# Seven block products for eight in one quad of each layer-A pair, with helper splits held back in ScalarE's queue

## The chip, the cores and the metric

One core of one Trainium2 chip runs the kernel. The metric is device time in microseconds (us) of one execution. The kernel before took 1844.6 us (median of three runs, 1844.6 to 1847.14). Engines are named as the profile names them: PE (TensorE, matmuls), PEld (its weight loads), ACT (ScalarE), DVE (VectorE), POOL (GpSimd) and SP (SyncE, here only an issuer of DMAs).

## The reference

Two layers over 256 tokens of width 2048, inner width 4096, 32 heads of 128, all in float32.

```python
h = rms_norm(x, a_norm)                       # layer A
q, k, v, g = split(h @ a_w_in, 4)             # 2048 -> 4 x 4096
o = chunked_relbias_attention(q, k, v)        # per head
x = x + (o * silu(g)) @ a_w_out               # 4096 -> 2048
h_kv = rms_norm(x, kv_norm)                   # layer B
k, v = split(h_kv @ kv_w, 2); logf = log_sigmoid(h_kv @ f_w + f_b)
q, g = split(rms_norm(x, b_norm) @ b_w_in, 2)
x = x + (forgetting_attention(q, k, v, cumsum(logf)) * silu(g)) @ b_w_out
return rms_norm(x, final_norm)
```

## The kernel before

**Units.** Every projection is cut into units of 512 output columns. In layer A a *pair* of units belongs to two heads (a group, `g` = 0 to 15): unit `aqk` gives their q and k, unit `avg` their v and gate. The contraction of 2048 is 16 blocks of 128, taken two at a time, so a unit has eight *steps*. A float32 product is made of three float32r products: x and w are each split into a high part (`xTh`, `aqk_hi`) and the rest (`xTl`, `aqk_lo`), and `mm3` (L160) issues hi·hi, hi·lo and lo·hi. With two tiles of 128 tokens (`NT`), a step is 2 x 2 x 3 = 12 matmuls of 128x512, a unit 96.

**The feed.** `Feed` (L171) streams the weights. SP loads a raw block pair of 512 KB (three slots, `RAW`), ACT copies it to the high part (L216), DVE subtracts to get the low part (L217), and both go into a ring of four (`SPLIT`): the split of step n+4 starts when PE has finished step n, and the load n+3 when DVE has finished split n.

**The side work.** The attention of a group is a generator (`attention`, L353) that `drive` (L519) advances at given steps of the units that run meanwhile (`QK_STEPS`, `PV_STEPS`). Its stages, in the order in which one group goes through them:

1. at the end of unit `aqk`: ACT scales q and k out of PSUM into `qk` (L335);
2. first step of `avg`: `turn` (L321) transposes 32x32 blocks on DVE into `qkY` and moves the blocks by 16 DMAs, all issued by POOL, into `qkZ`;
3. late in `avg`: the turned rows are split on ACT and DVE (`wideh`, `widel`, `q1h`, `q1l`, `q0`), then PE makes the scores `s1p`, `s0p` after the last step of `avg`;
4. in the next group's `aqk`: softmax on DVE and ACT (`sg`), times the gate, a second `turn` (`sgY`, 16 DMAs of POOL, `sgZ`), and `wideh`, `widel` again;
5. after the first step of the next `avg`: PE multiplies by v (`op`), DVE by the gate (`oT`, L409), ACT and DVE split it into `oAh`, `oAl`.

`qkZ` and `sgZ` share one buffer, so POOL cannot start stage 2 of a group before `oT` of the group before has read `sgZ`.

**Order.** Each engine's queue is in order. The order in a queue is set by a scheduler that takes the program's dependences and its own estimate of times; instructions that wait for nothing late may be placed ahead of others that stand earlier in the source.

Of the kernel before, what the change touches and what calls it, by code (L numbers as in the profile page):

```python
# [9 lines left out]
F32 = mybir.dt.float32  # L10
# [53 lines left out]
def trunk(ctx, tc, x, x_t, gains, a_w_in, a_rel, a_w_out, kv_w, f_w, f_b, b_w_in, b_w_out, final_norm, out):  # L64
# [94 lines left out]

    def mm3(acc, lhs, k, ts, hi, lo, nk):  # L160

        parts = [(lhs.h(k), hi), (lhs.h(k), lo), (lhs.l(k), hi)]
        steps = [(t, i) for t in ts for i in range(3)]
        if k < KB:
            steps = [(t, i) for i in (0, 2, 1) for t in ts]
        for t, i in steps:
            x, w = parts[i]
            pe.matmul(acc[t], x[:, t * P:(t + 1) * P], w,  # L168
                      start=k == 0 and i == 0, stop=k == nk - 1 and i == 2)

    class Feed:  # L171
# [20 lines left out]
        def begin(self, first=None):  # L192
            spec, b = next(self.todo, (None, 0))
            if spec:
                load, *splits = self.also.get((spec["name"], b), (None, None, None))
                if load:
                    load()
                self.loaded.append((spec, b, self.load(spec, b, first), splits))

        def prepare(self, ahead=True, parts=(slice(None),)):  # L200
            if not self.loaded:
                self.begin()
            if not self.loaded:
                return
            spec, b, raw, (before, behind) = self.loaded.pop(0)
            if before:
                before()
            nm, h = spec["name"], b - (spec["nk"] // KB - spec["late"])
            if 0 <= h < spec["kept"]:
                both = big_tile([P, 2, KB, UN], F32R, f"{nm}_keep{b}")  # L210
                hi, lo = both[:, 0], both[:, 1]
            else:
                hi = stream.tile([P, KB, UN], F32R, name=f"{nm}_hi{b}", tag="hi", bufs=SPLIT)
                lo = stream.tile([P, KB, UN], F32R, name=f"{nm}_lo{b}", tag="lo", bufs=SPLIT)
            for j in parts:
                act.activation(hi[:, j], raw[:, j], AF.Copy)  # L216
                self.splits.append(dve.tensor_sub(lo[:, j], raw[:, j], r32(hi[:, j])))  # L217
            if behind:
                behind()
            self.ready.append((hi, lo))  # L220
            while ahead and len(self.loaded) < RAW:
                n = len(self.loaded)
                self.begin()
                if len(self.loaded) == n:
                    break

        def fill(self):
# [18 lines left out]
    for g in range(NG):  # L246
        qkvg.append(spec(f"aqk{g}", a_w_in[2 * g], KD))
        qkvg.append(spec(f"avg{g}", a_w_in[2 * g + 1], KD))
    woven = [(qkvg[u], b) for u, b in WOVEN]
    todo = woven + [i for i in whole(qkvg[1]) if i not in woven]  # L250
    ao = [spec(f"ao{u}", a_w_out[u], KI) for u in range(4)]
    for sp_ in qkvg[2:] + ao:
        todo += whole(sp_)
# [13 lines left out]
    class Unit:  # L267
# [3 lines left out]
        def __init__(self, lhs, sp_):  # L271
            self.lhs, self.nk, self.late = lhs, sp_["nk"], sp_["late"]
            self.acc = [ps_acc.tile([P, UN], F32, name=f"{sp_['name']}_acc{t}", tag="acc") for t in range(NT)]
            self.held, self.left = [], self.nk // KB

        def step(self, b):
            hi, lo = feed.get()
            hold = b >= self.nk // KB - self.late
            if hold:
                self.held.append((b, hi, lo))  # L280
            for j in range(KB):
                mm3(self.acc, self.lhs, b * KB + j, range(1 if hold else NT), hi[:, j], lo[:, j], self.nk)
            self.left -= 1
            if not self.left:
                for b, hi, lo in self.held:
                    for j in range(KB):
                        mm3(self.acc, self.lhs, b * KB + j, [1], hi[:, j], lo[:, j], self.nk)

# [31 lines left out]

    def turn(src, n, name, queues=(pool, pool)):  # L321

        y = att.tile([P, NQ, n, SQ], F32, name=f"{name}Y", tag="Y")
        dve.transpose(y, src.rearrange("p n (j u) -> p j n u", u=SQ))  # L326
        z = att.tile([P, NQ, n, SQ], F32, name=f"{name}Z", tag="Z")
        for i in range(NQ):
            for j in range(NQ):
                queues[j % 2].dma_start(out=z[j * SQ:(j + 1) * SQ, i], in_=y[i * SQ:(i + 1) * SQ, j])  # L330
        return z
# [4 lines left out]

    def split(srcs, tag):
# [14 lines left out]

    def attention(g, biases, qk, vg, half, ocat, queues=(pool, pool)):  # L353

# [84 lines left out]

    for i in range(EXTRA):  # L440
        both = big_tile([P, 2, KB, UN], F32, name=f"early{i}")
        feed.early += [both[:, 0], both[:, 1]]
    xT = Stat("xT", KD)
    xr, homes = {}, iter(["wideh", "tb", "widel", "oT", "gs", "R", "Y", "Z", "wideh"])
    sq = [big_tile([P, BIG, S], F32, name=f"sq{i}") for i in range(KD // BIG)]

# [46 lines left out]
    oA = Stat("oA", KI)  # L493

    def side_a(g, accs):
        tb = att.tile([P, HG, S], F32, name="tb", tag="tb")
# [9 lines left out]
        qk = rows(UN, "qk")  # L506
        evac_scaled(accs["qk"], 0, UN, rsA, qk)
        yield
# [3 lines left out]

        yield from attention(g, biases, qk, vg, halfA, oA, (pool, pool) if g else (pool, act))

    def close_vg(accs):
        accs["v"] = v_split(accs["vg"], 0, rsA)
        accs["g"] = gate_from(accs["vg"], GC, halfA)
# [23 lines left out]
    for g in range(NG):  # L541
        accs = {}
        if g:
            accs["qk"], vg = drive(unit(xT), prev, PV_STEPS), unit(xT)
        else:
# [4 lines left out]
        advance(prev)  # L550
        accs["vg"] = drive(vg, prev, QK_STEPS if g else {0: 1, 5: 1, 6: 2}, old=old)
        close_vg(accs)
# [249 lines left out]
```

## Time and profile before

| what | value |
|---|---|
| median of three runs | 1844.6 us (1844.6 to 1847.14) |
| the profiled execution | 1843.38 us |
| its span | 1841.7 us |
| PE busy | 1830.1 us, 99% |
| PEld busy | 1523.0 us, 83% |
| DVE busy | 1121.7 us, 61% |
| ACT busy | 1005.6 us, 55% |
| POOL busy | 543.5 us, 30% |
| DMA | 396 MB, mean 215 GB/s |
| granted PE clock | 0.999 |

PE's share is near the whole span, but the records of matmuls overlap (each is shown with some 390 ns and the next starts earlier), so the price of a matmul is the distance between starts and not its duration. The other engines work beside PE; for them the question is at which moment in a group's round of some 46 us their result is wanted.

### The profile page before, as it was taken

How to read it: one execution, taken by the hardware profiler on the slowest of the kernel's cores; microseconds unless marked ns; L12 is line 12 of the kernel's file. 1: busy time of each engine (PE TensorE's matmuls, PEld its weight loads, DVE VectorE, ACT ScalarE, POOL GpSimd, SP SyncE). 2: the span in 40 equal slices, each digit the busy share in tenths (PEclk: the TensorE clock that was granted, in tenths of full speed). 3: DMA queues.
4: the chain of work that ended last, by engine and by line, in shares of the span. 5: the costliest groups of instructions: out<-in, count | busy, mean ns of one | idle time of the engine just before them, and what ended most of it. 6: DMA issues, size and time to landing. Idle time of an engine off the chain costs nothing.

```text
span 1841.7 us, 25094 instructions
## 1 busy us (share of the span) xinstructions
PE 1830.1 (99%) x8387; PEld 1523.0 (83%) x8387; DVE 1121.7 (61%) x1433; ACT 1005.6 (55%) x1695; POOL 543.5 (30%) x1127
## 2 busy tenths in 40 slices
PE   9999999999999999999999999999999999999998
PEld 7888888888888888888888888888888888888886
DVE  6666666666666666556655566666665666665654
ACT  6555555555555555454546565555555655554443
POOL 1333333333333333111103333333333333333000
PEclk9999999999999999999999999999999999999999
DMA  7766666666767666677756666666766766677664
GB/s 255 235 217 214 212 214 215 214 213 212 216 214 214 215 214 214 209 226 227 230 190 220 214 216 213 214 214 215 217 212 213 220 213 210 215 237 220 206 205 161
DMA packets 142241, 396.31 MB, mean 215 GB/s; under 512 B 31104, under 2 KB 35744, under 8 KB 141984
## 3 DMA queue, kind: packets, MB, share of 16 engines
q1 hardware_dynamic: 106960, 354.25, 61.6%
q0 software_dynamic: 34048, 39.13, 6.5%
q8 instruction: 66, 1.08, 0.3%
q10 hardware_dynamic: 1104, 1.34, 0.2%
q14 instruction: 63, 0.52, 0.1%
HBM read 351.05 MB, written 4.23 MB: 193 GB/s over the span
## 4 chain that ended last, share of the span: by engine, by line
PE 97%; DVE 1%; DMA 1%; ACT 0%; issue 0%; ACTq 0%; SPq 0%; DVEq 0%
PE bkv_acc L168 19%; PE bqg_acc L168 19%; PE avg_acc L168 18%; PE aqk_acc L168 18%; PE bo_acc L168 9%; PE ao_acc L168 9%; PE op L405 1%; PE s0p L371 1%; PE op L351 0%; PE s1p L351 0%; PE s1p L350 0%; PE op L350 0%; PE op L349 0%; PE s1p L349 0%; DMA avg_raw<-in_a_w_in 0%; DMA xr<-in_x_t 0%
## 5 line engine op out<-in xcount | busy, mean ns | idle before, releaser
L330 POOL DMA_DIRECT2D sgZ<-sgY x512 | 251.5, 498 | 435.2 <-DVE sgY L326 364.1
L330 POOL DMA_DIRECT2D qkZ<-qkY x504 | 247.9, 499 | 399.1 <-DVE vl L424 147.2
L217 DVE TENSOR_TENSOR bqg_lo<-bqg_raw,bqg_hi 128x1024 fp32r<-128x1024 f32 x128 | 156.0, 1222 | 121.3 <-ACT bqg_hi L216 121.3
L217 DVE TENSOR_TENSOR avg_lo<-avg_raw,avg_hi 128x1024 fp32r<-128x1024 f32 x127 | 154.0, 1219 | 110.8 <-ACT avg_hi L216 105.4
L217 DVE TENSOR_TENSOR bkv_lo<-bkv_raw,bkv_hi 128x1024 fp32r<-128x1024 f32 x128 | 155.6, 1219 | 87.6 <-ACT bkv_hi L216 87.6
L216 ACT ACTIVATE bqg_hi<-bqg_raw 128x1024 fp32r<-128x1024 f32 x128 | 135.3, 1058 | 128.3 <-PE bqg_acc L168 67.8
L217 DVE TENSOR_TENSOR aqk_lo<-aqk_raw,aqk_hi 128x1024 fp32r<-128x1024 f32 x125 | 151.5, 1219 | 84.6 <-ACT aqk_hi L216 84.5
L168 PE MATMUL aqk_acc<-aqk_hi,xTh 128*128 128x512 f32 x512 | 195.8, 392 | 0.5 <-ACT aqk_hi L216 0.5
L168 PE MATMUL bkv_acc<-bkv_hi,xkvh 128*128 128x512 f32 x512 | 195.7, 392 | 0.0
L168 PE MATMUL avg_acc<-avg_hi,xTh 128*128 128x512 f32 x512 | 195.7, 392 | 0.0
L168 PE MATMUL bqg_acc<-bqg_hi,xbh 128*128 128x512 f32 x512 | 195.5, 392 | 0.0
L216 ACT ACTIVATE avg_hi<-avg_raw 128x1024 fp32r<-128x1024 f32 x127 | 133.1, 1057 | 113.3 <-PE avg_acc L168 54.2
L168 PE MATMUL aqk_acc<-aqk_lo,xTh 128*128 128x512 f32 x512 | 194.1, 389 | 0.5 <-DVE aqk_lo L217 0.5
L168 PE MATMUL avg_acc<-avg_lo,xTh 128*128 128x512 f32 x512 | 194.1, 389 | 0.4 <-DVE avg_lo L217 0.4
L168 PE MATMUL bkv_acc<-bkv_hi,xkvl 128*128 128x512 f32 x512 | 194.4, 390 | 0.0
L168 PE MATMUL aqk_acc<-aqk_hi,xTl 128*128 128x512 f32 x512 | 194.4, 390 | 0.0
L168 PE MATMUL bqg_acc<-bqg_hi,xbl 128*128 128x512 f32 x512 | 194.3, 390 | 0.0
L168 PE MATMUL avg_acc<-avg_hi,xTl 128*128 128x512 f32 x512 | 194.3, 390 | 0.0
L168 PE MATMUL bkv_acc<-bkv_lo,xkvh 128*128 128x512 f32 x512 | 194.1, 389 | 0.0
L168 PE MATMUL bqg_acc<-bqg_lo,xbh 128*128 128x512 f32 x512 | 194.1, 389 | 0.0
L216 ACT ACTIVATE bkv_hi<-bkv_raw 128x1024 fp32r<-128x1024 f32 x128 | 134.8, 1057 | 76.2 <-PE bqg_acc L168 61.3
L216 ACT ACTIVATE aqk_hi<-aqk_raw 128x1024 fp32r<-128x1024 f32 x125 | 131.0, 1056 | 81.4 <-PE aqk_acc L168 40.1
(188 smaller groups left out, 3430.3 us busy)
## 6 DMA issues: line engine op xcount, KB each, us to landing
bqg_raw<-in_b_w_in SPq DMA_DIRECT2D x128, 512.0 KB, 4.2
bkv_raw<-in_kv_w SPq DMA_DIRECT2D x128, 512.0 KB, 3.5
avg_raw<-in_a_w_in SPq DMA_DIRECT2D x127, 512.0 KB, 4.3
aqk_raw<-in_a_w_in SPq DMA_DIRECT2D x125, 512.0 KB, 3.8
ao_raw<-in_a_w_out SPq DMA_DIRECT2D x64, 512.0 KB, 4.4
bo_raw<-in_b_w_out SPq DMA_DIRECT2D x64, 512.0 KB, 4.2
sgZ<-sgY POOLq DMA_DIRECT2D x512, 40.0 KB, 4.0
qkZ<-qkY POOLq DMA_DIRECT2D x504, 32.0 KB, 3.3
```

Source lines behind the costliest of these rows:

```text
L168: pe.matmul(acc[t], x[:, t * P:(t + 1) * P], w, start=k == 0 and i == 0, stop=k == nk - 1 and i == 2)
L216: act.activation(hi[:, j], raw[:, j], AF.Copy)
L217: self.splits.append(dve.tensor_sub(lo[:, j], raw[:, j], r32(hi[:, j])))
L330: queues[j % 2].dma_start(out=z[j * SQ:(j + 1) * SQ, i], in_=y[i * SQ:(i + 1) * SQ, j])
L371: pe.matmul(s0p[:, i], q0[:, i], qkT[:, HG + i, 0], start=True, stop=True)
L405: pe.matmul(op[:, i, P:], v1[:, i * DH:(i + 1) * DH], pT[:, i, NT], start=False, stop=i == HG - 1)
```

## The change

In the last two blocks of the contraction, a pair of units is a product of a 2x2 grid of x blocks (two blocks of the contraction, two token tiles) and a 2x2 grid of weight blocks (two blocks, units `aqk` and `avg`): eight block products of three matmuls each. The new kernel does this *quad* for groups 1 to 15 with seven products of sums and differences (Winograd's form of Strassen's scheme). Each unit then has seven steps, and the quad's four parts stand after the third step of `aqk`.

```diff
+QK7_STEPS = {0: 1, 5: 1, 6: 2}
+PV7_STEPS = {0: 1, 6: 1}
+QUAD = 7
+QUAD_STEP = 3
...
-            while ahead and len(self.loaded) < RAW:
+            if ahead:
+                self.refill()
+
+        def refill(self):
+            while sum(raw is not None for _, _, raw, _ in self.loaded) < RAW:
...
+        def load_quad(self, g):
+            raw, t = quad_raw, quad_t
+            for r in range(2):
+                self.behind(raw[:, r, :, :1], -1)
+                sp.dma_start(out=raw[:, r], in_=a_w_in[2 * g + r][QUAD])
+            dve.tensor_sub(t[:, 0], raw[:, 1], raw[:, :, 0])
+            dve.tensor_sub(t[:, 1, 0], raw[:, 1, 1], t[:, 0, 0])
+            dve.tensor_sub(t[:, 1, 1], raw[:, 0, 1], t[:, 1, 0])
+
+        def quad(self, i):
+            raw, t = quad_raw, quad_t
+            src = [raw[:, 0], t[:, 0], raw[:, 1, 1:], t[:, 1]][i]
+            n = src.shape[1]
...
+            act.activation(hi[:, :n], src, AF.Copy)
+            dve.tensor_sub(lo[:, :n], src, r32(hi[:, :n]))
+            self.ready.append((hi, lo))
+
+        def behind(self, dst, n):
+            act.activation(dst, r32(self.ready[n][0][:, :, :1]), AF.Copy)
...
-    def turn(src, n, name, queues=(pool, pool)):
+    def turn(src, n, name, queues=(pool,) * NQ):
...
-                queues[j % 2].dma_start(out=z[j * SQ:(j + 1) * SQ, i], in_=y[i * SQ:(i + 1) * SQ, j])
+                queues[j].dma_start(out=z[j * SQ:(j + 1) * SQ, i], in_=y[i * SQ:(i + 1) * SQ, j])
...
+        if place is not None:
+            feed.behind(hi[:, :, :1], place)
...
-        kh, kl = split([qkT[:, HG + i] for i in range(HG)], "wide")
-        qh, ql = split([qkT[:, i, 1:] for i in range(HG)], "q1")
+        kh, kl = split([qkT[:, HG + i] for i in range(HG)], "wide", line[0])
+        qh, ql = split([qkT[:, i, 1:] for i in range(HG)], "q1", line[0])
...
+        if line[0] is not None:
+            feed.behind(q0[:, :, :1], line[0])
...
+    def quad(qk, vg):
...
+        p1, p5, p7, p6 = (bank(n) for n in ("p1", "p5", "p7", "p6"))
+        w = feed.get()
+        prod(p1, x(0, 0), w, 0, True)
+        prod(qk.acc[0], x(1, 0), w, 1, False)
+        w = feed.get()
+        prod(p5, sx(0), w, 0, True)
+        prod(p7, sx(2), w, 1, True)
+        w = feed.get()
+        dot3(vg.acc[0], sx(3), [v[:, 0] for v in w], True, False)
+        vg.begun.add(0)
+        w = feed.get()
+        prod(p6, sx(1), w, 0, True)
+        prod(qk.acc[1], x(1, 1), w, 1, False)
+        act.activation(comb[:, 0], p1, AF.Copy)
+        dve.tensor_add(comb[:, 3], comb[:, 0], p6)
+        dve.tensor_add(comb[:, 2], comb[:, 3], p5)
+        dve.tensor_add(comb[:, 1], comb[:, 3], p7)
+        dve.tensor_add(comb[:, 3], comb[:, 1], p5)
+        for t in range(NT):
+            act.activation(comb[:, t], comb[:, t], AF.Copy, scale=rsA[:, t:t + 1])
...
-        evac_scaled(accs["qk"], 0, UN, rsA, qk)
+        if g:
+            for t in range(NT):
+                dve.scalar_tensor_tensor(qk[:, t], accs["qk"][t], rsA[:, t:t + 1], comb[:, t],
+                                         op0=OP.mult, op1=OP.add)
+        else:
+            evac_scaled(accs["qk"], 0, UN, rsA, qk)
...
-        yield from attention(g, biases, qk, vg, halfA, oA, (pool, pool) if g else (pool, act))
+        yield from attention(g, biases, qk, vg, halfA, oA, (pool, pool, pool, act), (2, 1))
...
+            for t in range(NT):
+                dve.tensor_add(comb[:, NT + t], accs["vg"][t], comb[:, NT + t])
```

`behind` writes two elements per partition of a buffer from a weight split that is already in the feed, so that ACT's later write of that buffer stands after that split in the queue. `sums_of_x` makes the four sums of x blocks once, after group 0. The buffers that held the first loads and the squares of x now also hold the quad's raw weights, its differences and the combined products (`quad0`, `quad1`, `comb`). The quad of group g+1 is loaded at the first step of `avg` of group g; four of the 16 DMAs that make `qkZ` are now issued by ACT.

The places on which the prediction rests, in group 6 and the start of group 7. First ACT's queue in unit `avg` of group 6, from the split of its third step to the turned rows of the scores (`wideh<-sgZ` are the turned weights of the softmax, `wideh<-qkZ` the turned keys). Before:

```order
L344 ACTIVATE wideh_2811<-sgZ_2668 128x256 x2
L216 ACTIVATE avg6_hi2_2793<-avg6_raw2_2743 128x1024
L335 ACTIVATE qk_2820<-aqk6_acc0_2639,rstd_a_387 128x512
L335 ACTIVATE qk_2820<-aqk6_acc1_2640,rstd_a_387 128x512
L216 ACTIVATE avg6_hi3_2825<-avg6_raw3_2761 128x1024
L216 ACTIVATE avg6_hi4_2877<-avg6_raw4_2779 128x1024
L413 ACTIVATE oAh1_176<-oT_2852 128x512
L216 ACTIVATE avg6_hi5_2895<-avg6_raw5_2797 128x1024
L216 ACTIVATE avg6_hi6_2913<-avg6_raw6_2829 128x1024
L216 ACTIVATE avg6_hi7_2931<-avg6_raw7_2881 128x1024
L216 ACTIVATE aqk7_hi0_2949<-aqk7_raw0_2899 128x1024
L344 ACTIVATE wideh_2985<-qkZ_2859 128x256 x2
```

And now:

```order
L264 ACTIVATE quad0_101<-avg6_hi3_2998 128x2 x2
L227 ACTIVATE avg6_hi4_3057<-avg6_raw4_2953 128x1024
L461 ACTIVATE oAh1_176<-oT_3025 128x512
L374 DMA qkZ_3032<-qkY_3030 32x256 x4
L227 ACTIVATE avg6_hi5_3075<-avg6_raw5_2971 128x1024
L227 ACTIVATE avg6_hi6_3093<-avg6_raw6_3002 128x1024
L227 ACTIVATE aqk7_hi0_3111<-aqk7_raw0_3061 128x1024
L227 ACTIVATE aqk7_hi1_3129<-aqk7_raw1_3079 128x1024
L264 ACTIVATE wideh_3147<-aqk7_hi1_3129 128x2
L264 ACTIVATE q1h_3154<-aqk7_hi1_3129 128x2
L264 ACTIVATE q0_3161<-aqk7_hi1_3129 128x2
L390 ACTIVATE wideh_3147<-qkZ_3032 128x256 x2
```

The two evacuations of `qk` are gone from ACT, four DMA issues and the two-element writes have come, and the turned keys now stand behind the second weight split of the next unit, where they stood behind its first.

Then DVE's queue in the next unit `aqk`, from the end of unit `avg` to the transpose of the softmax weights (`sgY`). Before:

```order
L217 TENSOR_TENSOR aqk7_lo2_3000<-aqk7_raw2_2935,aqk7_hi2_2999 128x1024
L424 SCALAR_TENSOR_TENSOR vl_3039<-avg6_acc0_2823,rstd_a_387,vh_3038 128x256
L378 SCALAR_TENSOR_TENSOR sg_3027<-s1p_3017,tb_2817 128x2x256
L378 SCALAR_TENSOR_TENSOR sg_3027<-s0p_3018,tb_2817 128x2x128
L379 TENSOR_REDUCE nm_3028<-sg_3027 128x2 x2
L436 SCALAR_TENSOR_TENSOR gs_3044<-gs_3044,avg6_acc0_2823 128x256
L436 SCALAR_TENSOR_TENSOR gs_3044<-gs_3044,avg6_acc1_2824 128x256
L217 TENSOR_TENSOR aqk7_lo3_3052<-aqk7_raw3_2953,aqk7_hi3_3051 128x1024
L387 RECIPROCAL csc_3069<-sm_3029 128x4
L388 TENSOR_TENSOR csc_3069<-csc_3069,half_a_389 128x4
L217 TENSOR_TENSOR aqk7_lo4_3096<-aqk7_raw4_2971,aqk7_hi4_3095 128x1024
L326 STREAM_TRANSPOSE sgY_3076<-sg_3027 128x1280
```

And now:

```order
L228 TENSOR_TENSOR aqk7_lo2_3165<-aqk7_raw2_3097,aqk7_hi2_3164 128x1024
L622 TENSOR_TENSOR comb_103<-avg6_acc0_2783,comb_103 128x512
L622 TENSOR_TENSOR comb_103<-avg6_acc1_2784,comb_103 128x512
L426 SCALAR_TENSOR_TENSOR sg_3192<-s1p_3182,tb_2992 128x2x256
L426 SCALAR_TENSOR_TENSOR sg_3192<-s0p_3183,tb_2992 128x2x128
L427 TENSOR_REDUCE nm_3193<-sg_3192 128x2 x2
L472 SCALAR_TENSOR_TENSOR vl_3206<-comb_103,rstd_a_387,vh_3205 128x256
L484 SCALAR_TENSOR_TENSOR gs_3211<-gs_3211,comb_103 128x256 x2
L259 TENSOR_TENSOR quad_lo0_3221<-quad0_101,quad_hi0_3220 128x1024
L435 RECIPROCAL csc_3236<-sm_3194 128x4
L436 TENSOR_TENSOR csc_3236<-csc_3236,half_a_389 128x4
L259 TENSOR_TENSOR quad_lo1_3263<-quad1_102,quad_hi1_3262 128x1024
```

Two additions into `comb` now stand ahead of the softmax, v and the gate are read from `comb`, and the quad's splits have the places of the unit's fourth and fifth. On PE the quad itself is this piece, between the third and the fourth step of `aqk`:

```order
L395 MATMUL p1_3294<-quad_hi0_3220,xTh1_106 128x512
L396 MATMUL p1_3294<-quad_lo0_3221,xTh1_106 128x512
L397 MATMUL p1_3294<-quad_hi0_3220,xTl1_108 128x512
L395 MATMUL aqk7_acc0_3216<-quad_hi0_3220,xTh1_106 128x512
L396 MATMUL aqk7_acc0_3216<-quad_lo0_3221,xTh1_106 128x512
L397 MATMUL aqk7_acc0_3216<-quad_hi0_3220,xTl1_108 128x512
L395 MATMUL p5_3295<-quad_hi1_3262,sums_104 128x512
L396 MATMUL p5_3295<-quad_lo1_3263,sums_104 128x512
L397 MATMUL p5_3295<-quad_hi1_3262,sums_104 128x512
L395 MATMUL p7_3296<-quad_hi1_3262,sums_104 128x512
L396 MATMUL p7_3296<-quad_lo1_3263,sums_104 128x512
L397 MATMUL p7_3296<-quad_hi1_3262,sums_104 128x512
```

behind which one product goes into the accumulator of `avg` (3 matmuls) and `p6` and one more product of `aqk` close the quad (6); its four parts have 6, 6, 3 and 6 matmuls where a step of the unit has 12.

More of the change, by code (lines that the diff above doesn't have):

```diff
@@ L168, in mm3 @@
             pe.matmul(acc[t], x[:, t * P:(t + 1) * P], w,
-                      start=k == 0 and i == 0, stop=k == nk - 1 and i == 2)
+                      start=t not in begun, stop=k == nk - 1 and i == 2)
+            begun.add(t)
     class Feed:
@@ L193, in begin @@
             spec, b = next(self.todo, (None, 0))
-            if spec:
+            if spec == "quad":
+                self.loaded += [(spec, i, None, (None, None)) for i in range(4)]
+            elif spec:
                 load, *splits = self.also.get((spec["name"], b), (None, None, None))
@@ L205, in prepare @@
             spec, b, raw, (before, behind) = self.loaded.pop(0)
+            if spec == "quad":
+                self.quad(b)
+                self.refill()
+                return
             if before:
@@ L397, in attention @@
         yield
-        ph, pl = split([pT[:, i, :NT] for i in range(HG)], "wide")
+        ph, pl = split([pT[:, i, :NT] for i in range(HG)], "wide", line[1])
         yield
@@ L511, in vg @@
             return accs["v"], accs["g"]
-        yield from attention(g, biases, qk, vg, halfA, oA, (pool, pool) if g else (pool, act))
+        yield from attention(g, biases, qk, vg, halfA, oA, (pool, pool, pool, act), (2, 1))
     def close_vg(accs):
+        if "quad" in accs:
+            for t in range(NT):
+                dve.tensor_add(comb[:, NT + t], accs["vg"][t], comb[:, NT + t])
+            accs["vg"] = [comb[:, NT + t] for t in range(NT)]
         accs["v"] = v_split(accs["vg"], 0, rsA)
@@ L543, in trunk @@
         if g:
-            accs["qk"], vg = drive(unit(xT), prev, PV_STEPS), unit(xT)
+            accs["quad"] = True
+            first, second = (Unit(xT, next(order)) for _ in range(2))
+            accs["qk"] = drive(rest(first), prev, PV7_STEPS, (QUAD_STEP - 1, lambda: quad(first, second)))
+            vg = rest(second)
         else:
```

59 lines of the change are left out of this document (46 added, 13 removed).

## Prediction

> **What bounds the kernel now.** I read the page's head, then windows of one group's round, then the chain that ended last.
>
> ```profile
> span 1841.7 us, 25094 instructions
> PE 1830.1 (99%) x8387; PEld 1523.0 (83%) x8387; DVE 1121.7 (61%) x1433; ACT 1005.6 (55%) x1695; POOL 543.5 (30%) x1127
> 304.40:350.00 45.60, 45.60 (x212) 38.09 (x211) 29.12 (x39) 26.27 (x46) 15.91 (x33) 1.00 0.69 213
> 0.00:35.00 35.00, 32.68 (x138) 24.77 (x139) 26.61 (x44) 26.04 (x44) 1.90 (x11) 1.00 0.80 277
> PE 97%; DVE 1%; DMA 1%; ACT 0%; issue 0%; ACTq 0%; SPq 0%; DVEq 0%
> 328.70 21.81 PE aqk_acc L168 x96
> 304.58 2.72 PE avg_acc L168 x12
> 350.51 2.72 PE avg_acc L168 x12
> ```
>
> In a round of layer A (the window from 304.40, group 6) PE has no gap, DVE works 29 and ACT 26 of 45.6 us; PE's few idle us lie in the first 35. The chain is PE for 97%. A unit of 96 matmuls takes 21.81 us, so a matmul costs 0.2272 us, a step of twelve 2.72. From one `avg` to the next (304.58 to 350.51) a round takes 45.93 us. The end is therefore PE's count of matmuls, as long as nothing reaches PE late.
>
> **What is removed.** Seven products for eight save three matmuls in each of 15 groups: 45 x 0.2272 = 10.2 us, all on PE, whose path sets the end. Against the profiled 1843.38 us that is 1833.2; the median of the runs is 1.2 us above that execution, so 1834.4.
>
> The Trainium skill, "TensorE: Matmul & The Clock Gate", section "Back-to-back issue gap", gives about 131 ns for a matmul with N=512 in a sustained stream; by that the saving would be an estimated 45 x 0.131 = 5.9 us. The trace does not agree (0.2272), and I take the trace.
>
> **What is added, and whether PE ever waits for it.** Durations from these groups:
>
> ```profile
> L217 DVE TENSOR_TENSOR aqk_lo<-aqk_raw,aqk_hi 128x1024 fp32r<-128x1024 f32 x125 | 151.5, 1219 | 84.6 <-ACT aqk_hi L216 84.5
> L216 ACT ACTIVATE aqk_hi<-aqk_raw 128x1024 fp32r<-128x1024 f32 x125 | 131.0, 1056 | 81.4 <-PE aqk_acc L168 40.1 <-PE avg_acc L168 29.2 <-DMA aqk_raw<-in_a_w_in 8.4
> L217 DVE TENSOR_TENSOR aqk_lo<-early,aqk_hi 128x512 fp32r<-128x512 f32 x6 | 4.0, 688 | 1.8 <-ACT aqk_hi L216 1.8
> L582 DVE TENSOR_TENSOR xin<-ao_acc,xin 128x512 f32<-128x512 f32 x8 | 5.1, 682 | 0.0
> L335 ACT ACTIVATE qk<-aqk_acc,rstd_a 128x512 f32<-128x512 f32 x32 | 20.7, 679 | 1.8 <-PE aqk_acc L168 1.8
> L731 ACT ACTIVATE fin<-ssq,part 128x1 f32<-128x1 f32 x2 | 0.6, 294 | 0.0
> 35.91 5.33 ACTq L330 DMA_DIRECT2D qkZ<-qkY  x8
> ```
>
> DVE per group: three differences (1.22 + 2 x 0.69 = 2.6); quad splits of three and a half blocks for two (1.83); six additions into `comb` (6 x 0.68 = 4.1); two evacuations of `qk` (1.4): 9.9, so 29 becomes 39 of 45.3. ACT: splits +1.7, `p1` 0.7, two scalings 1.4, less two evacuations 1.4; six two-element writes at 0.19 to 0.29 each (bounds: an accumulator read, 190 ns, and the 294 above) 1.1 to 1.8; and four DMA issues, which hold ACT for 5.33 / 8 = 0.67 each, 2.7: about 6.5, so 26 becomes 33. Neither becomes the bound by its sum. Weight bytes are the same. The start (first squares and loads share buffers) I cost at 0, bounds -0.5 and +2 of the 2.3 idle us in the first window.
>
> The order of work is another matter, because each group's attention is a loop through ACT, DVE and POOL's DMAs that must close once per round. One round of it before:
>
> ```profile
> 304.14 0.72 ACT L344 ACTIVATE wideh<-sgZ 128x256 fp32r<-128x256 f32 x2 [3.90 <-DMA sgZ<-sgY]
> 305.85 1.23 DVE L217 TENSOR_TENSOR avg_lo<-avg_raw,avg_hi 128x1024 fp32r<-128x1024 f32 x1 [0.50 <-ACT avg_hi L216]
> 304.42 0.62 PE L168 MATMUL avg_acc<-avg_hi,xTh 128*128 128x512 f32 x2
> 310.40 0.75 DVE L409 TENSOR_TENSOR oT<-op,sgZ 128x256 f32<-128x256 f32 x2
> 311.18 0.63 ACT L413 ACTIVATE oAh<-oT 128x512 fp32r<-128x512 f32 x1 [2.32 <-DVE oT L409]
> 311.77 7.93 POOL L330 DMA_DIRECT2D qkZ<-qkY  x16 [11.00 <-PE avg_acc L168]
> 323.19 0.72 ACT L344 ACTIVATE wideh<-qkZ 128x256 fp32r<-128x256 f32 x2 [2.65 <-DMA qkZ<-qkY]
> 325.60 2.36 DVE L217 TENSOR_TENSOR aqk_lo<-aqk_raw,aqk_hi 128x1024 fp32r<-128x1024 f32 x2 [0.80 <-ACT aqk_hi L216]
> 327.38 0.28 PE L349 MATMUL s1p<-wideh,q1h 128*128 128x256 f32 x1
> 328.37 0.69 DVE L378 SCALAR_TENSOR_TENSOR sg<-s1p,tb 128x512 f32<-128x512 f32 x1
> 328.97 0.41 DVE L378 SCALAR_TENSOR_TENSOR sg<-s0p,tb 128x256 f32<-128x256 f32 x1
> 329.31 1.00 DVE L379 TENSOR_REDUCE nm<-sg 128x2 f32<-128x512 f32 x2
> 330.22 0.74 DVE L436 SCALAR_TENSOR_TENSOR gs<-gs,avg_acc 128x256 f32<-128x256 f32 x2
> 332.02 0.17 DVE L387 RECIPROCAL csc<-sm 128x4 f32<-128x4 f32 x1
> 332.78 1.27 ACT L392 ACTIVATE sg<-gs,csc 128x128 f32<-128x128 f32 x4
> 334.08 1.51 DVE L326 STREAM_TRANSPOSE sgY<-sg 128x1280 f32<-128x1280 f32 x1
> 348.19 0.72 ACT L344 ACTIVATE wideh<-sgZ 128x256 fp32r<-128x256 f32 x2 [2.03 <-DMA sgZ<-sgY]
> 563.70 1.51 DVE L326 STREAM_TRANSPOSE sgY<-sg 128x1280 f32<-128x1280 f32 x1
> 580.31 0.73 ACT L344 ACTIVATE wideh<-sgZ 128x256 fp32r<-128x256 f32 x2 [4.48 <-DMA sgZ<-sgY]
> 701.50 1.51 DVE L326 STREAM_TRANSPOSE sgY<-sg 128x1280 f32<-128x1280 f32 x1
> 714.02 0.72 ACT L344 ACTIVATE wideh<-sgZ 128x256 fp32r<-128x256 f32 x2 [0.38 <-DMA sgZ<-sgY]
> aqk_raw<-in_a_w_in SPq DMA_DIRECT2D x125, 512.0 KB, 3.8
> DMA to landing us min/median/max: 3.1/3.8/8.2
> ```
>
> Call W the start of `wideh<-sgZ`. Before: W to `wideh<-qkZ` 19.05 (304.14 to 323.19), on to `sgY` 10.89, on to the next W 14.1; together 44.05, of a round of 45.93. The keys' splits are done 1.6 after 323.19, at 324.8; PE wants them at 327.38: 2.6 to spare.
>
> Now, the same legs:
>
> - *W to the keys.* `oT` ended 7.0 after W; the two evacuations that DVE now does ahead of it add 2 x 0.62 (0.60 lies between the starts 328.37 and 328.97): 8.25. POOL then issues 12 DMAs for 16, 5.95 for 7.93, and with the 0.6 ahead and 3.5 behind that the rows show (311.77 less 311.15; 323.19 less 319.70) the turn lands at W + 18.3. But the split now stands behind the second weight split of the next unit, whose slot is freed by step six of `avg`, which on ACT stands behind `oAh` and the four DMA issues: 8.3 + 0.65 + 2.7 + 1.06 + 1.22 = 13.9, load 3.8 and 0.1, split 1.06, three two-element writes 0.6: W + 19.5. The second is later and counts.
> - *Keys to `sgY`.* Until `lo2` is done 3.6 (325.60 + 1.17 less 323.19); two additions into `comb` 1.2; softmax additions and maxima 0.94 + 0.91; `vl` and gate 1.05; `quad_lo0` 1.15; reciprocal and product 0.4; ACT's scaling 1.28: 10.5.
> - *`sgY` to W.* In the 15 groups before 14.6 on the mean, 12.5 (701.50) to 16.6 (563.70); unchanged.
>
> New waits are in these legs: the additions into `comb` wait for the end of `avg` and the softmax stands behind them on DVE; ACT's scaling of `comb` waits for the additions behind the quad, and `aqk`'s last split stands behind that, but its load, which needs the slot of the fourth step, lands only at T1 + 16.4 (below) and PE wants it at 21.
>
> Sum 44.6. PE's round becomes 45.93 - 0.68 = 45.25. So 1.9 us of slack shrink to about 0.6: the loop still closes inside PE's round, barely. PE waits for the scores when W is later than 0.7 before the first matmul of `avg` (304.42 in the rows): the keys' splits are ready at W + 20.9, and PE arrives one step sooner than before, at 327.38 - 304.42 - 2.72 = 20.2. Before, W lay between 3.8 ahead of that first matmul (714.02) and 0.3 behind it (580.31, rounds of 45.93 apart); with 0.6 to gain back each round W drifts ahead of the limit, and only after long returns such as 580.31 does PE wait a us or so. I add 1.6 us in all for those: 1836.0.
>
> The quad itself: four splits for 6 + 6 + 3 + 6 = 21 matmuls, 4.77 us, where DVE alone needs 4.3. Split n+4 starts when step n frees its slots, which shows in this row (the step ended two steps ahead of 304.42, at 298.98):
>
> ```profile
> 299.17 1.06 ACT L216 ACTIVATE avg_hi<-avg_raw 128x1024 fp32r<-128x1024 f32 x1 [1.66 <-PE aqk_acc L168]
> ```
>
> 0.19 later to start, 1.10 to DVE, 1.23 there: 2.55 from slot to ready. From the unit's start (T1), step three ends at 8.16, the fourth part's low half is ready at 10.7, wanted at 11.8; the fourth step's slot comes free at 9.52, `p1`'s evacuation (0.68) stands ahead of it on ACT, low half 12.4, wanted 13.15. Spare 0.7, if DVE has done `sgY` and `quad_lo2` by 9.5, that is if `sgY` starts by T1 + 7.4 or, with the spare, 8.0. That is the same loop: W later by a us takes both margins.
>
> Else hidden: the quad's load and differences (done some 14 us into `avg`, wanted 15 later); the additions behind the quad (two steps early); PSUM banks `p1` to `p6`, read by T1 + 17.5, next wanted at 26.5; SP, which waits for the same splits as before.
>
> **Rivals.**
>
> - *The loop is longer than PE's round (slower).* Place: the keys' split. If the second weight block lands in 6 us instead of 3.8 (of these loads the longest took 8.2), or the four DMA issues hold ACT 2 us longer in all, the loop takes 46.6 to 46.8 and sets the round. At 46.8: 1834.4 + 15 x 1.55 = 1858. It decides at 45.93, 1.3 us above my sum. For it: the slack is smaller than what such a sum can err. Against it: SP loads nothing for some 7 us around the quad, which should shorten the return of `sgZ`.
> - *Small waits in most rounds.* My sum 0.3 to 0.8 short, or the quad's short steps catching DVE behind `sgY`: 0.3 to 0.6 a group, 5 to 9 us, 1839 to 1844.
> - *DVE holds POOL off.* The added subtractions read two SBUF operands; if they delayed POOL's DMA issues by half of one in two, 12 x 0.3 for the keys (of which 1.2 are hidden) and 16 x 0.3 for the weights, the loop would be 44.6 + 2.4 + 4.8 = 51.8 and the time 1834.4 + 15 x 6.55, about 1933. Against: with DVE busy 64% of the round POOL's issue took 498 ns as minimum and median and 514 at most:
>
> ```profile
> L330 POOL DMA_DIRECT2D sgZ<-sgY x512: 498/498/514, 61.3 to 1698.2; - x171
> ```
>
>   The Trainium skill, "SBUF — State Buffer", section "Who interferes with whom", has such instructions contend with GpSimd instructions that read SBUF, though not with ones that only write; this row shows none of it.
> - *The saving is not there:* a matmul behind a new bank or a sum's weights costs more than 0.2272. Nothing in the rows speaks for it.
>
> **How the numbers follow.** Forecast (0 to 4 us of waits, 1834 to 1838.5) 0.60; small waits 0.22, half of it under 1840.9; waits near the saving, 0.06; the longer loop 0.09; POOL held off 0.02; no saving 0.01. A measurement of this kernel can tell about 0.2%, 3.7 us, from no change: faster means under 1840.9, slower over 1848.3. Faster 0.60 + 0.11 = 0.71; same 0.11 + 0.06 + 0.01 = 0.18; slower 0.09 + 0.02 = 0.11. The range 1833 to 1845 leaves out the slower cases, half of the 0.06 and a little below, some 0.17.
>
> **What would show it.** Right: matmul starts 0.227 apart through the quad, rounds of 45.25 us, PE busy 1820, no idle before `s1p`, `p6` or the fourth step. The loop: rounds above 45.25, PE idle before `s1p` released by ACT or DVE (`wideh`, `q1l`), `wideh<-qkZ` directly behind a late `aqk_hi`. The quad: PE idle released by `quad_lo` or the fourth step's `aqk_lo`. POOL: issues far above 498 ns. I am wrong if the legs above are off by a us, which I cannot see for ACT's DMA issues beside other work and for the small writes.

## The result, and the profile after

The changed kernel takes 1856.8 us (median of 10 runs, 1850.4 to 1861.6) where the kernel before takes 1845.7 (1843.6 to 1849.2): a ratio of 1.0057, 95% interval 1.0042 to 1.0072. It is slower by 0.6%; the forecast was 1836.0, with a range up to 1845. The profiled execution of the changed kernel took 1855.79 us, its span is 1854.1, against 1841.7 before. Two executions at a granted clock of 0.58 and 0.56, one of the kernel before (2989.4 us) and one of e3 below (3084.2), are in none of the times and ratios.

The head of the page after:

```profile
span 1854.1 us, 25445 instructions
PE 1832.2 (99%) x8342; PEld 1517.0 (82%) x8342; DVE 1256.9 (68%) x1634; ACT 1058.4 (57%) x1835; POOL 516.0 (28%) x1071
```

And windows of one round (group 9's scores to group 10's) and of the start, with each engine's busy time in the page's order, then the granted clock, the DMA engines' share and GB/s:

```profile
473.69:519.84 46.15, 45.90 (x209) 38.08 (x210) 37.76 (x52) 28.78 (x54) 13.89 (x29) 1.00 0.68 219
0.00:35.00 35.00, 33.24 (x138) 25.30 (x139) 26.78 (x45) 25.78 (x44) 2.52 (x11) 1.00 0.81 276
```

There are 45 matmuls fewer (8342 for 8387), and yet PE is busy 2 us longer: records of matmuls overlap, so one that waits inside a row of matmuls lengthens "busy" and not "idle". The round is 46.15 us where PE's matmuls alone would take 45.25. Where the time goes is read from distances between starts. From the start of one group's scores (`s1p`) to the next, the 15 rounds before take 45.93 each. After, their median is 46.16 (46.26 without the first one), and three stand out: 51.83, 48.05 and 47.19. From the first scores to the last that is 699.7 us for 689.0. The start costs nothing (first scores at 51.25 us for 51.78), and some 2 us are lost behind layer A; their cause stays open.

Which wait it is shows in one round of the changed kernel, group 8 to group 9, in the order of time (timeline; the last bracket is the idle time before and who ended it):

```profile
451.45 0.72 ACT L390 ACTIVATE wideh<-sgZ 128x256 fp32r<-128x256 f32 x2 [0.71 <-DMA sgZ<-sgY]
454.83 0.38 SPq L246 DMA_DIRECT2D quad<-in_a_w_in  x1
457.24 0.42 SPq L246 DMA_DIRECT2D quad<-in_a_w_in  x1
459.01 0.75 DVE L457 TENSOR_TENSOR oT<-op,sgZ 128x256 f32<-128x256 f32 x2
459.79 0.63 ACT L461 ACTIVATE oAh<-oT 128x512 fp32r<-128x512 f32 x1 [2.44 <-DVE oT L457]
459.80 2.45 ACTq L374 DMA_DIRECT2D qkZ<-qkY  x4
460.38 3.91 POOL L374 DMA_DIRECT2D qkZ<-qkY  x8 [13.03 <-DVE oT L457]
465.18 1.23 DVE L247 TENSOR_TENSOR quad<-quad 128x1024 f32<-128x1024 f32 x1 [4.02 <-DMA quad<-in_a_w_in]
466.27 2.08 POOL L374 DMA_DIRECT2D qkZ<-qkY  x4 [1.98 <-DMA qkZ<-qkY]
466.32 1.22 DVE L228 TENSOR_TENSOR avg_lo<-avg_raw,avg_hi 128x1024 fp32r<-128x1024 f32 x1
471.14 1.06 ACT L227 ACTIVATE aqk_hi<-aqk_raw 128x1024 fp32r<-128x1024 f32 x1 [3.06 <-DMA aqk_raw<-in_a_w_in]
472.71 0.72 ACT L390 ACTIVATE wideh<-qkZ 128x256 fp32r<-128x256 f32 x2
473.69 0.39 PE L395 MATMUL s1p<-wideh,q1h 128*128 128x256 f32 x1 [0.58 <-ACT q1h L390]
474.39 0.38 PE L397 MATMUL s1p<-wideh,q1l 128*128 128x256 f32 x1 [0.15 <-DVE q1l L391]
483.24 1.51 DVE L370 STREAM_TRANSPOSE sgY<-sg 128x1280 f32<-128x1280 f32 x1
497.67 0.72 ACT L390 ACTIVATE wideh<-sgZ 128x256 fp32r<-128x256 f32 x2
```

PE stands at the scores until the keys' splits come, one by one: 0.98 us after `wideh<-qkZ` starts, the first matmul can go. W to the keys is 21.26 here (forecast 19.5), keys to `sgY` 10.53 (10.5), `sgY` to the next W 14.43 (14.6). The loop of this round is 46.22, longer than PE's 45.25. Over the groups the three legs average 20.79, 10.52 and 15.33 (the last without group 0's), and W comes every 46.71 us from group 0's to group 14's.

Two waits inside the first leg stand beside the quad's load, which SP issued at 454.83 and 457.24. DVE stands 4.02 us at the head of its queue for that load, and behind it stands the split that frees the slot for the next unit's second block. POOL issues eight DMAs and then waits 1.98 us for the first of them to land. DMA in 5-us windows of the same round, and in the last row one window of a turn of the keys in the kernel before:

```profile
430.00:435.00 5.00, 5.00 (x24) 4.14 (x23) 4.89 (x11) 4.79 (x16) 0.20 (x1) 1.00 0.40 120
435.00:440.00 5.00, 5.00 (x24) 4.14 (x23) 4.74 (x6) 4.35 (x7) 2.77 (x6) 1.00 0.12 33
455.00:460.00 5.00, 5.00 (x26) 4.18 (x26) 4.76 (x7) 1.27 (x2) 0.00 (x0) 1.00 0.83 277
460.00:465.00 5.00, 5.00 (x24) 4.14 (x23) 0.69 (x1) 2.55 (x3) 3.91 (x8) 1.00 0.92 316
455.00:460.00 5.00, 5.00 (x24) 4.14 (x23) 2.45 (x2) 1.67 (x2) 3.32 (x7) 1.00 0.99 269
```

Around the quad, which needs no block of the feed, the DMA share falls to 0.12; when the keys' turn starts, at 460, it is 0.92: the quad's 1 MB is in flight beside the feed's blocks. One window proves little, as the 0.99 of the kernel before shows. But over the 15 turns the DMA share in the first 5 us from POOL's first DMA is 0.83 on the mean, for 0.73 before, and this first DMA takes 5.53 us from issue to landing, for 3.67. The waits over the whole layer, of DVE and (from 50 to 760 us) of POOL, with the sum, the number and the longest; the last row is POOL's before:

```profile
DVE quad L247 <- DMA quad<-in_a_w_in: 42.7, 14, 4.3
POOL qkZ L374 <- DMA qkZ<-qkY: 26.2, 14, 2.8
POOL qkZ L330 <- DMA qkZ<-qkY: 5.3, 9, 1.6
```

### The profile page after: what moved, and what is told of

Read it like the earlier page. It is cut to its first block, busy times and chain, and to the rows that moved or that the text cites. A ratio compares the mean times of both kernels' runs of the same rounds, so it can differ in the third digit from the quotient of the medians.

```text
span 1854.1 us, 25445 instructions
## 1 busy us (share of the span) xinstructions
PE 1832.2 (99%) x8342; PEld 1517.0 (82%) x8342; DVE 1256.9 (68%) x1634; ACT 1058.4 (57%) x1835; POOL 516.0 (28%) x1071
## 4 chain that ended last, share of the span: by engine, by line
PE 62%; DMA 1%; issue 0%; ACT 0%; POOL 0%; DVE 0%; ACTq 0%; POOLq 0%
PE bqg_acc L172 19%; PE bkv_acc L172 18%; PE bo_acc L172 9%; PE ao_acc L172 8%; PE avg_acc L172 2%; PE aqk_acc L172 2%; DMA xinZ<-xinY 1%; DMA sgZ<-sgY 0%; PE s0p L419 0%; PE op L453 0%; PE s1p L397 0%; PE op L396 0%; PE s1p L395 0%; PE op L397 0%; PE s1p L396 0%
## 5 line engine op out<-in xcount | busy, mean ns | idle before, releaser
L374 POOL DMA_DIRECT2D qkZ<-qkY x448 | 219.8, 498 | 460.5 <-DVE vl L472 142.1
L172 PE MATMUL avg_acc<-avg_lo,xTh 128*128 128x512 f32 x452 | 171.5, 391 | 3.8 <-DVE avg_lo L228 3.8
L172 PE MATMUL avg_acc<-avg_hi,xTh 128*128 128x512 f32 x452 | 173.0, 394 | 0.0
L172 PE MATMUL aqk_acc<-aqk_hi,xTh 128*128 128x512 f32 x452 | 172.9, 394 | 0.0
L172 PE MATMUL avg_acc<-avg_hi,xTl 128*128 128x512 f32 x452 | 171.7, 391 | 0.0
L172 PE MATMUL aqk_acc<-aqk_lo,xTh 128*128 128x512 f32 x452 | 170.9, 390 | 0.5 <-DVE aqk_lo L228 0.5
L172 PE MATMUL aqk_acc<-aqk_hi,xTl 128*128 128x512 f32 x452 | 171.2, 390 | 0.0
L228 DVE TENSOR_TENSOR avg_lo<-avg_raw,avg_hi 128x1024 fp32r<-128x1024 f32 x112 | 136.3, 1218 | 45.4 <-ACT avg_hi L227 43.7
L227 ACT ACTIVATE aqk_hi<-aqk_raw 128x1024 fp32r<-128x1024 f32 x110 | 114.6, 1054 | 77.3 <-DMA aqk_raw<-in_a_w_in 73.5
L228 DVE TENSOR_TENSOR aqk_lo<-aqk_raw,aqk_hi 128x1024 fp32r<-128x1024 f32 x110 | 133.3, 1223 | 35.2 <-ACT aqk_hi L227 34.5
```

Source lines behind the costliest of these rows:

```text
L172: pe.matmul(acc[t], x[:, t * P:(t + 1) * P], w, start=t not in begun, stop=k == nk - 1 and i == 2)
L374: queues[j].dma_start(out=z[j * SQ:(j + 1) * SQ, i], in_=y[i * SQ:(i + 1) * SQ, j])
```

## The experiments

Three theories stood against each other. D: DVE's wait for the quad's load makes the next blocks and so the keys late. C: the load crowds the DMA engines just when the keys turn. K: the place of the keys' split, behind the second weight split, is the cause whatever the load does. e2 leaves out the quad's loads of groups 2 to 15, which use group 1's weights; e3 also drops the two-element writes that held the load back. For the first four, the edits were:

```diff
 e1  load_quad: load as before; the three differences go into diffs(), called three steps later:
+        def diffs(self):
+            self.behind(t[:, 0, :, :1], -1)      # behind avg's seventh split
+            dve.tensor_sub(t[:, 0], raw[:, 1], raw[:, :, 0])
...
 e2  load_quad:
+                if g == 1:
                     sp.dma_start(out=raw[:, r], in_=a_w_in[2 * g + r][QUAD])
 e3  differences as in e1, and the load of group g+1 right behind quad(first, second) of group g:
+    QUAD_STEP - 1, lambda: (quad(first, second), g + 1 < NG and feed.load_quad(g + 1)),
+    3, lambda: g + 1 < NG and feed.diffs()
 e4
-    (pool, pool, pool, act), (2, 1))
+    (pool, pool, pool, act), (None, 1))
```

> The three differences of the quad's weights stand behind the split of avg's seventh step on DVE (one two-element write on ACT, 0.2 us, holds them there); the load itself stays where it is. Theory D (DVE stands at the head of its queue for the quad's load, 42.7 us in 14 rounds, 3.0 each, and the splits behind it, the load that needs their slot and the keys' split come late): that wait goes, W to the keys falls from 20.8 to 19 to 19.8, rounds to 45.3 to 45.9, time 1836 to 1846. Theory C (the quad's 1 MB is bunched with the regular loads while the turn of the keys runs, and everything lands late): the landings stay at 4.2 to 5.7 us, W to the keys stays above 20.3, time 1851 to 1857. Theory K (the place of the keys' split behind the second weight split): as C, 1851 to 1857.

> The quad's weights are loaded for group 1 alone; groups 2 to 15 use group 1's again (the loads of 14 groups are left out, all other work is there). Theories D and C: no wait for the load and no bunching, 1834 to 1841, and by C alone clearly below what moving the differences gives. Theory K: the keys' split still stands behind the second weight split, 1848 to 1857.

> The next quad is loaded right after this group's quad has read its buffer, where the DMA engines are at 12 to 40% in the rounds after the change, and its differences stand late in unit aqk where DVE has a gap of 2.7 us. Theories D and C: 1834 to 1842, W to the keys 18.5 to 19.5; the return of sgZ may become 0.5 to 1 longer, since its DMAs now run beside the quad's load. Theory K: 1848 to 1857.

> The turned keys, q1 and q0 are not held behind the second weight split (three two-element writes go); the scheduler puts them behind the first. Theory K: W to the keys falls to 19 and the time to 1837 to 1846. Theories D and C: DVE's wait of 3 us and the late turn stay; the keys' split gains at most the distance between the turn's landing and the second weight split, under 1 us a round, time 1844 to 1857.

Times with ratios to executions of the kernel before beside each, POOL's wait in the keys' turn, the mean legs (W to the keys, keys to `sgY`, `sgY` to W) and the median round, the last three from the traces as above (third leg and round without group 0's):

| kernel | us | ratio, 95% interval | POOL's wait | legs | round |
|---|---|---|---|---|---|
| before | 1845.7 | | 5.3 | 19.64, 11.64, 14.57 | 45.93 |
| after | 1856.8 | 1.0057 (1.0042 to 1.0072) | 26.2 | 20.79, 10.52, 15.33 | 46.26 |
| e1 | 1854.0 | 1.0050 (1.0034 to 1.0066) | 29.0 | 20.65, 10.51, 15.43 | 46.28 |
| e2 | 1841.5 | 0.9985 (0.9976 to 0.9995) | 2.9 | 19.62, 10.53, 15.49 | 45.25 |
| e3 | 1840.7 | 0.9977 (0.9967 to 0.9987) | 10.7 | 19.52, 10.52, 15.82 | 45.29 |
| e4 | 1872.0 | 1.0149 (1.0133 to 1.0165) | 23.0 | 20.45, 11.65, 15.45 | 47.50 |

e1 refutes D as the only cause. DVE's wait is gone, but the keys' split now waits for the turn. Where it had stood directly behind `aqk_hi` in 8 of 14 rounds, ACT now stands idle for `qkZ` in 14 of 15. ACT's waits for the turn have grown from 31.9 us in 18 to the first row below, and POOL's wait has not shrunk (second row):

```profile
ACT wideh L394 <- DMA qkZ<-qkY: 46.7, 30, 5.5
POOL qkZ L378 <- DMA qkZ<-qkY: 29.0, 16, 3.2
```

e2 and e3 bear out C. Whether the load is left out or only moved to where the engines were idle, the first leg falls by 1.2 and 8 of 15 rounds fall to 45.25, which is exactly PE's own. POOL's first DMA lands after 2.13 us in e2 and 2.37 in e3, where it took 5.53 in the changed kernel and 5.69 in e1. (e2's time lies just above the 1841 that was expected at most. The means of the rounds are 45.63 and 45.74, so the full saving does not show in either.) In one round of e3 the load of the next quad starts just ahead of this quad's matmuls, these start 0.23 apart, and POOL waits 0.31 where it had waited 1.98 (timeline, from the load to the splits of the next keys):

```profile
470.45 4.02 SPq L245 DMA_DIRECT2D quad<-in_a_w_in  x2
473.65 0.39 PE L400 MATMUL aqk_acc<-quad_hi,xTl 128*128 128x512 f32 x1
473.88 0.39 PE L398 MATMUL p<-quad_hi,sums 128*128 128x512 f32 x1
474.11 0.39 PE L399 MATMUL p<-quad_lo,sums 128*128 128x512 f32 x1
500.88 1.47 POOL L377 DMA_DIRECT2D qkZ<-qkY  x3 [0.31 <-DMA qkZ<-qkY]
506.42 0.72 ACT L393 ACTIVATE wideh<-qkZ 128x256 fp32r<-128x256 f32 x2 [1.02 <-DMA qkZ<-qkY]
```

The Trainium skill, "DMA: Bandwidth & Descriptors", section "Queues, rings and completion order", has each DMA engine go round the queues that have work for it, a packet from each at a time. By that, SP's blocks and POOL's small DMAs delay each other whichever engine issued them. The traces agree as far as they go: the same bytes cost the turn 26.2 us of waiting at one place and 10.7 at another. How the packets of the two queues take turns, no run here shows.

e4 refutes K and turns it round: by the ratios the hold is worth some 17 us, and 1872 lies above all that was expected. Without it the keys' split stands in front of the second weight split, keys to `sgY` becomes 11.65 (that split comes in between), and the keys come hardly sooner (20.45 for 20.79), since they wait for the turn.

The last run, made after the others, raises the dose. The load comes one step of `avg` later (`(0, lambda: ...load_quad...)` becomes `(1, ...)`):

> The kernel after with the quad's load one step of avg later, so that more of its 1 MB is in flight while POOL issues the turn of the keys; its differences then stand behind the splits of avg's last steps by the scheduler's order, so DVE does not wait for the load ahead of them. Crowding theory (the load beside the turn makes the first of its DMAs land late, POOL waits for them before its ninth, and the keys come late): POOL's wait grows from 1.9 a round to 2.5 to 4, W to the keys from 20.8 to 21.3 to 23, the time 1860 to 1885. If only the sum of bytes counts, or DVE's wait for the load, it is 1850 to 1857 as after or as with the later differences.

It took 1863.0 us, ratio 1.0096 (1.0079 to 1.0112): the legs are 21.15, 10.51 and 15.58, the median round 47.11. DVE's wait for the load has halved and POOL's has grown:

```profile
DVE quad L247 <- DMA quad<-in_a_w_in: 20.9, 14, 2.5
POOL qkZ L374 <- DMA qkZ<-qkY: 42.5, 17, 4.0
```

POOL's first DMA now lands after 6.62 us. So where only the place of the load and its differences changes (after, e1, e2, e3, e12), time follows POOL's wait and not DVE's, but for differences of 1 to 3 us. (W to the keys stayed just under what was expected, 21.3 to 23.)

Next, ACT's part in the turn, and the return from `sgY` to W. e5 to e7 let SP issue four or eight of the 16 DMAs of `sgZ` (in e6 and e7 on top of e3), e8 gives POOL back all 16 of `qkZ`:

```diff
 e5, e6
+    (pool, pool, pool, act), (2, 1), (pool, pool, pool, sp))
 e7
+    (pool, pool, pool, act), (2, 1), (pool, pool, sp, sp))
 e8
+    (pool,) * 4 if g else (pool, pool, pool, act), (2, 1))
```

> The kernel after, with 4 of the 16 DMAs that make sgZ issued by SP (idle at that time) for POOL; nothing else changes. Loop theory (the side work's loop of 46.7 us sets the round, whichever leg is long): the return from sgY to W gets 1 to 2 shorter (15.3 to 13.5 to 14.5), the loop 44.8 to 45.7, the time 1838 to 1846, although the quad's load stays bunched. Rival (PE loses its time in waits that the quad's load makes directly: DVE behind the load, splits late for PE): 1852 to 1857.

> The early load of the quad and its late differences, with 4 of the 16 DMAs of sgZ issued by SP. Loop theory: the loop of 45.9 that the early load left falls by 1 to 2, below PE's 45.25, PE waits for nothing in layer A and the whole saving of 10.2 us shows: 1833 to 1837. Rival (something else holds PE, or the quad's matmuls cost more than 0.2272 each): stays at 1839 to 1842.

> As the early load with 8 of the 16 DMAs of sgZ issued by SP. Loop theory: once the loop is below PE's round a shorter leg brings nothing more, so the same as with 4 within 2 us (1833 to 1837); a rival by which the time follows the return's length: 2 to 10 us less than with 4. SP's issues (0.33 to 0.6 each) may hold back the second half of the quad's load and the seventh step's by 2 us, which would cost up to 5.

> The kernel after, with all 16 DMAs that make qkZ issued by POOL in groups 1 to 15, as before the change (ACT issues none). Loop theory: POOL's turn becomes 2 us longer (4 x 0.5), the turned keys land at W plus 22 to 23, the loop becomes 48 to 49 and the time 1873 to 1890. Rival (ACT's four issues of 0.6 each delay the feed and are the loss): 1840 to 1850.

| kernel | us | ratio, 95% interval | POOL's wait | legs | round |
|---|---|---|---|---|---|
| e5 | 1856.7 | 1.0069 (1.0052 to 1.0086) | 27.2 | 21.51, 10.52, 14.68 | 46.16 |
| e6 | 1848.9 | 1.0021 (1.0010 to 1.0032) | 12.6 | 20.06, 10.52, 15.88 | 46.50 |
| e7 | 1866.1 | 1.0114 (1.0099 to 1.0129) | 10.0 | 20.47, 10.52, 16.71 | 47.63 |
| e8 | 1876.5 | 1.0169 (1.0149 to 1.0190) | 13.9 | 21.80, 10.51, 15.49 | 47.74 |

e8's time is as expected (W to the keys, 21.80, just under its 22 to 23): ACT's four issues are worth 20 us, and ACT's issues were not the loss. The other three missed. In e5 POOL is done with `sgZ` 2 us sooner, yet W comes only 0.65 sooner: in all 15 rounds W follows half a us behind `avg`'s second weight split, behind which the change holds it, and not behind a landing. In e6 and e7 SP itself pays. It waits for `sgY` at the head of its queue, with the feed's blocks behind it:

```profile
SPq L377 <- DVE sgY L373: 41.1, 16, 4.6
```

The return gets longer (15.88, 16.71). The loop theory as I had put it, that any leg can be cut for itself, is wrong here: the return ends at the feed.

Three runs then tried to shorten the return. e9 is e3 with the quad's parts in another order, so that the next load starts sooner. e11 adds to e9 that W stands ahead of `avg`'s second weight split. e10 is the changed kernel without the low halves of the last two parts (their high halves stand in):

```diff
 e9
-            src = [raw[:, 0], t[:, 0], raw[:, 1, 1:], t[:, 1]][i]
+            src = [raw[:, 0], raw[:, 1, 1:], t[:, 0], t[:, 1]][i]
 e10
+            if i in (2, 3):
+                lo = hi
 e11  PV7_STEPS {0: 1, 4: 1}, line (2, -1), and in prepare:
+                act.activation(hi[:, :, :1], r32(self.after[:, :, :1]), AF.Copy)   # after = wideh
```

> The early load of e3, with the quad's four parts in the order first, third, second, fourth (6, 3, 6 and 6 matmuls), so that its buffer has been read some 3 us sooner and the next quad's load starts where the DMA engines are idle, ahead of the seventh step's load. By the crowding theory avg's first loads land sooner, the second weight split of avg, behind which the return's split is held, comes sooner, and the return falls from 15.8 by 0.5 to 1.2; the loop goes to 44.8 to 45.4 and the time to 1833 to 1839. If the return is set by DVE's work behind sgY alone and not by the loads, it stays at 15.5 to 15.9 and the time at 1839 to 1842.

> The kernel after; the low parts of the quad's third and fourth parts are left out (their high parts stand in for them in the matmuls), which takes 1.85 us of DVE from behind sgY. If the return hangs on the feed (DVE's splits behind sgY free the slots of avg's first loads, and the return's split is held behind avg's second weight split), the return falls from 15.3 by 0.8 to 1.5, until the turn's own landing ends it, the loop to 45.3 to 45.9 and the time to 1838 to 1848. If the return is set by its own 16 DMAs, it stays within 0.3 of 15.3 and the time at 1853 to 1857.

> As e9, with the return's split held behind avg's first weight split and ahead of the second (the second waits for it through a two-element write). If the hold behind the second split is what ends the return, it falls to 14.2 to 14.9 (then the turn's landing ends it), the loop is below 45.25 and the time 1832 to 1837, equal to or below e9. If avg's second split then comes too late for PE (it waits for the return's landing, PE wants it some 5 us after W), single waits cost up to 5: 1837 to 1842.

e9 and e11 missed, and e10 came out on its second branch. e9: 1846.0 us, 1.0006 (0.9997 to 1.0015), legs 19.54, 10.94, 15.59; the return gained 0.2, and keys to `sgY` lost 0.4, since the order of the parts also moved DVE's split of the third one between the reciprocal and its product. e10: 1856.4, 1.0063 (1.0048 to 1.0077), return 15.47; so it does not hang on DVE's work behind `sgY`. e11: 1855.6, 1.0054 (1.0039 to 1.0068), return 15.12; W now waits about 1.2 us for the landing, and the first leg is 20.59, because `avg`'s splits, which had been ahead of W, now delay `oT` by 0.9 (W to `oT` 8.11 for 7.25). Landing and hold lie within a us of each other, and taking one away leaves the other. In the changed kernel itself it is the hold that ends most returns: W starts 0.35 us behind `avg`'s second weight split in 12 of 15 rounds, and ACT stands idle for the landing of `sgZ` only twice between 50 and 775 us, where it did so 16 times before. What makes landing and split late, and so the return 0.5 to 1.2 longer than before, stays open.

e3 is the version that beats both kernels: 0.9977 of before.

## A pause that had been hidden

The three long rounds of the changed kernel have one thing in common. POOL's rows show, in both kernels, a pause of 2.2 to 2.9 us for nothing that the profile knows, and each of the three rounds holds one. Before; after; e3:

```profile
225.52 3.92 POOL L330 DMA_DIRECT2D qkZ<-qkY  x8 [2.69 <-issue]
405.72 6.37 POOL L330 DMA_DIRECT2D qkZ<-qkY  x13 [2.87 <-issue]
574.10 2.94 POOL L330 DMA_DIRECT2D sgZ<-sgY  x6 [2.87 <-issue]
```

```profile
253.43 3.90 POOL L374 DMA_DIRECT2D sgZ<-sgY  x8 [2.74 <-issue]
445.88 1.47 POOL L374 DMA_DIRECT2D sgZ<-sgY  x3 [2.30 <-issue]
651.33 2.94 POOL L374 DMA_DIRECT2D qkZ<-qkY  x6 [2.61 <-issue]
```

```profile
247.81 3.91 POOL L377 DMA_DIRECT2D sgZ<-sgY  x8 [2.74 <-issue]
```

Counted in POOL's DMAs from the start of the program, it comes after the 128th and then after every 121st, to the end of the program (in the kernel before at 225, 405, 574, 753, 1052 us and on, in the kernel after at 253, 445, 651, 897, 1151). The counts are the same in all 14 traces, also in e5 to e7, where POOL issues fewer DMAs and the pauses come later. Before, no round is longer for it: W came up to 3.8 us ahead of PE. After, the first of these falls into group 4's return (18.91 us), and a round of 51.83 follows. In e3 the same place gives the only long round, 48.47; the pause at 437 falls into a round of 45.25 and the one at 638 into one of 46.16. In e2 the pause at 247 costs nothing, and the longest round, 47.81, holds the one at 636. In e5 the two longest rounds, 49.40 and 48.64, hold the pauses at 515 and 278. But in e7 the longest, 50.41, holds none. So a pause goes with most of the long rounds; it was not moved by itself to show that it makes them.

## Why the prediction was wrong

- **The saving** was right: seven products for eight give rounds of 45.25, reached wherever the loop lets PE (e2, e3, and the shortest rounds of the kernel after, 45.25 and 45.43). The quad's short steps make PE wait for nothing: from scores to `op` at best 27.73 us, the 25.69 of before less 2.72 plus 21 x 0.2272.
- **W to `oT` and keys to `sgY`** were right: 7.59 (forecast 7.5, as 8.25 less `oT`'s 0.75) and 10.52 (10.5). The work that the change adds to DVE was priced well. (One slip: by the prediction's own 1.6 for the keys' splits they are ready at W + 21.1 and not W + 20.9, which moves the limit for W by 0.2 and no more.)
- **The step that failed is W to the keys**, 20.79 for 19.5, and in it the line "Else hidden: the quad's load and differences". I had costed their end ("some 14 us into `avg`, wanted 15 later") and not what they stand beside, so that they cost nothing in the sum; they cost 1.2 us a round. The turn was to be there at W + 18.3, with 5.95 for POOL's 12 DMAs and 3.5 behind them; measured from `oAh`, POOL is done after 8.46 for 6.55, and the last DMA lands at W + 19.9 on the mean. The hold was to end at 19.5, with the second block's load issued at 13.9 and taking 3.8; the load took 3.66 but was issued at 15.2, behind DVE's wait of 3.0 a round (in e1, without that wait, at 13.5), which puts the hold's end near 20.5. Both ways were late, which is why taking one of them away brought so little (in e1 the turn lands at 20.3). Without the load (e2) the leg is 19.62 for the forecast 19.5, and that agreement is in part luck: there the split waits for the turn, which lands at W + 19.1, and not for the hold that the sum counted.
- **"`sgY` to W unchanged"** failed by 0.7. "SP loads nothing for some 7 us around the quad, which should shorten the return" did not come true. The landing no longer ended it; in 12 of 15 rounds the hold behind `avg`'s second split did, which the change gives it and which I left uncosted.
- **"+1.6 for long returns"** was mis-sized for the loop that came: with no slack, the rounds above the median of 46.26 alone cost 5.6 + 1.8 + 0.9 = 8.3.
- **The first rival** had the place and the price: it said 46.6 to 46.8 and, at 46.8, 1858; measured 46.71 and 1856.8, and its sign, the keys' split directly behind a late `aqk_hi`, shows in 8 of 14 rounds. But neither of its two mechanisms is what happened. The second block's load took 3.66 us on the mean and 3.99 at most, not 6; it was late because it was issued late. ACT's issues were not longer than assumed (0.61 us median for 0.67). The price is in part luck too, since it holds the three long rounds and the 2 us behind layer A, which the rival did not count. Its chance of 0.09 was too small for a sum that left 0.6 us of slack with two unpriced terms. POOL's issues took 496 ns (498 before), so the third rival is out.

The account of the two profiled executions closes: 15 rounds at 1.01 above 45.25 (the median of 46.26) make 15 us, the rounds beyond that 5.8 more, together 20.9 of lost time against a saving of 10.2; with 2 behind layer A and -0.5 at the start that gives 12.2 of the 12.4 us between the spans.

## What to carry to other kernels

When work is removed from the engine that bounds a kernel, the next loop takes over, and its slack has to be priced with everything that the change puts beside it. A transfer that lands long before it is wanted is not free: look at whose DMAs share the place where it runs, and at how long these take to land there. The DMA share of one window does not tell it: 0.99 did no harm before. And ask what a queue's head waits for: a "hidden" operation in an in-order queue holds up all that stands behind it, as DVE's differences did here and SP's issues in e6.

## What was not expected of the hardware

POOL's DMA issue pauses for about 2.7 us after its 128th DMA and then after every 121st (most of them of 32 partitions), in every trace of this case; why stays open. And 1 MB of loads beside a turn of 12 + 4 DMAs of 32 KB makes its first DMA land after 5.53 us, for 2.13 without the loads (e2), and POOL done 1.6 us later (8.46 behind `oAh` for 6.91), though the DMA share over a round is 0.68.
